# Half of four merge blocks issued beside the last attention rows, as a stream of lowest rank

## The chip, the cores and the metric

The kernel runs on one core of one Trainium2 chip. The metric is the device time of one execution in microseconds (us). Five engines work side by side, each on its own queue of instructions in program order: TensorE (PE: matrix products and transposes), VectorE (DVE), ScalarE (ACT), GpSimd (POOL) and SyncE (SP, which here issues most DMAs). They wait for one another through semaphores. A wait holds up everything behind it in the same queue.

## The reference, cut to what matters

One layer of a hybrid block over 512 tokens (528 with 16 meta tokens), width 1024, all in float32. Names as in the reference:

```
u = rmsnorm(h); proj = u @ w_in
gates  = sigmoid(proj[..., C_RW + C_FX:] + b_gate)
y_rw   = rwkv7_branch(...)     # recurrent half, 512 wide
y_fx   = fox_branch(...)       # causal attention with forget gates, 512 wide
merged = gates[:D] * (y_rw @ w_out_rw) + gates[D:] * (y_fx @ w_out_fx)
h = h + merged @ w_o
z = rmsnorm(h); h = h + square(relu(z @ w_up)) @ w_down
```

The change concerns `merged`: sixteen products of a 128-column block of `w_out_rw` or `w_out_fx` with one branch's output, each times its gate.

## The kernel before, in words

Every large product is made in three passes over operands that are split in two, `hi` (a rounded copy, made by ACT) and `lo` (the remainder, made by DVE): `hi*hi + hi*lo + lo*hi` (`passes`, `split`, `load_h`). A weight block is loaded by SP in two halves of 128x512 into `wraw` and split into `whi` and `wlo`; each of the three has a ring of four buffers.

*Front.* Up to the end of `turns.run()` the recurrent branch, the attention, the input projections and the sums of the later weights run as streams, Python generators that yield before a group of matmuls. `Turns.run` keeps a modelled PE time and takes the first stream, in order of rank, whose condition is met. That fixes the order of PE; the order on the other engines is fixed by the scheduler of the framework, which puts an instruction where its own model says that its inputs are ready. The gate blocks are the lowest projections: `gate_job` evacuates a product to `gt` and stores it to DRAM (`gates_d`, tile `gd`). Attention goes through four pairs of heads `p`, and in each through four rows of 128 queries `i`: `scored` (products `psc`, the mask and the row minimum on DVE, Exp on ACT, the scaling by `rsum` on DVE), `turned` (transposes `ppt`, `ppm`, copied to `pT`, `pTm`) and `mixed` (products `py`, copied to `y_fx`). For each row there are two heads, so two of each. `group_norm` ends the recurrent branch and writes `y_rw`.

*Merge.* After the front, `y_rw` and `y_fx` are split into `yhi`, `ylo` (eight blocks `k`, four of each branch). For each of eight output blocks `m` both weight halves are loaded, and for each branch `br` the gate is fetched (`gl`), ACT takes its Tanh, PE makes 12 matmuls into a PSUM bank `po` (4 blocks `k` by 3 passes), DVE multiplies, POOL adds the two branches, and the sum is split into `mhi`, `mlo`. That is 192 matmuls of 128x128 by 512 columns. The product with `w_o` follows (first `L1096`, then `L1113`), then the MLP (`L1143`, `L1233`).

`uhi`, `ulo` hold the normalised input, which only the projections read. Before, they live in a pool that ends with the front, and `yhi`, `ylo` take other memory (tags `zhi`, `zlo`).

Of the kernel before, what the change touches and what calls it, by code (L numbers as in the profile page):

```python
# [9 lines left out]
F32 = mybir.dt.float32  # L10
F32R = mybir.dt.float32r
# [15 lines left out]
KB = 8  # L27
CDEC = math.exp(-0.5)
SLICES = (4, 6, 6)
FIRST = (0, 4, 10)  # L30


# [118 lines left out]
class Turns:  # L151
# [1 line left out]

    ROOM = {0: 0.0, 1: 0.8, 2: 1.5, 3: 1.5, 4: 2.5, 8: 0.5, -1: 0.0}

    def __init__(self, tc, clock):
        self.tc, self.clock, self.streams, self.count = tc, clock, [], 0
# [29 lines left out]
def kernel(ctx, tc, ht, x, win, par, cst, gain, lora, wout, wo, wup, wdn, out, dbg=None):  # L189
# [6 lines left out]
    def dump(name, ap):  # L196
        if name in dbg:
            nc.sync.dma_start(dbg[name], ap)
# [60 lines left out]
    def split(hi, lo, x):  # L259
        A.copy(hi, x)  # L260
# [7 lines left out]
    quarters = [[wdn[i][256 * c:256 * c + 256] for c in range(8)] for i in range(4)]  # L268
    tsum = [[dr.tile([256, 512], F32, name=f"tsum{i}") for c in range(8)] for i in range(4)]

    with ExitStack() as st:
        up = st.enter_context(tc.tile_pool(name="up", bufs=1))
        ps = st.enter_context(tc.tile_pool(name="ps", bufs=2, space=PSUM))

        def ppj(name="ppj"):
# [160 lines left out]
            return job, raws  # L436

        converted = []

        def convert(job, raws):  # L440
            low = V if len(converted) < 2 else G
# [10 lines left out]
        def projections(total):  # L452
            fetched, done = None, 0
            while done < total:
                if fetched is None:
                    yield lambda: 0.0 if jobs else math.inf
                    fetched = fetch(jobs.pop(0))
                cur = convert(*fetched)
                fetched = fetch(jobs.pop(0)) if jobs else None
                while cur is not None:  # L460
                    (_, _, _, begin, parts, ev, need), w = cur
                    nxt = convert(*fetched) if fetched else None
                    fetched = fetch(jobs.pop(0)) if jobs else None
                    if need is not None:
                        yield need
                    evac = begin()
                    for a0, a1 in parts:
                        po = None
                        n = 0
                        for k in range(KB):  # L470
                            if k % 2 == 0 or a1 - a0 > 300:
                                yield lambda f=po is None: max(ck.ready(*w[k // 4]), ck.ring("pj", 1, 2) if f else 0.0)
                            if po is None:
                                po = ppj("pj")[:, :a1 - a0]
                            for a, b in passes(wk(w, k), U):
# [5 lines left out]
                    cur = nxt  # L481

        def gate_job(i):
            def begin():
# [514 lines left out]
        def weight_sums():  # L999

            def part(t, c):
                return t[c].rearrange("(a b) c -> a (b c)", b=2)

            def behind(dma, engine):
                x = next(x for x in reversed(nc.cur_bb.bb.instructions) if str(x.engine).endswith(engine) and x.name != dma.ins.name)
                tc.add_manual_dep(dma.ins, x.name, mybir.DependencyInfo(mybir.DependencyClass.NoSync, mybir.DependencyReason.DATA),
                                  reason="spread over the front")

            t1, t2, t3, t4 = tsum
            b11, b12, b22, b21 = quarters  # L1010
            steps = []
            for c in range(8):
                for a, b in (((t1, b11), (t1, b12)), ((t3, b12), (t3, b22)), ((t2, b22), (t2, t1)), ((t4, b21), (t4, t2))):
                    steps += [(*a, c, False), (*b, c, True)]
            for n in range(1, len(steps) - 2, 2):
                steps[n], steps[n + 1] = steps[n + 1], steps[n]
            for n, (dst, src, c, adds) in enumerate(steps):
                yield lambda: 45.0 + 6.0 * n
                if adds:
                    behind(nc.gpsimd.dma_start(part(dst, c), part(src, c), accum_op=ALU.add, max_dma_last_dim=2048), "Pool")  # L1020
                else:
                    behind(nc.scalar.dma_start(part(dst, c), part(src, c), max_dma_last_dim=2048), "Activation")
# [12 lines left out]
    hres = hp.tile([128, 4, 1024], F32, name="hres")  # L1035
    yhi = hp.tile([128, KB, S], F32R, name="yhi", tag="zhi")
    ylo = hp.tile([128, KB, S], F32R, name="ylo", tag="zlo")
    ps = ctx.enter_context(tc.tile_pool(name="ps2", bufs=4, space=PSUM))

    def ppo():  # L1040
# [4 lines left out]

    with ExitStack() as st:
        mp = st.enter_context(tc.tile_pool(name="mp", bufs=1))
        for j, src in enumerate((y_rw, y_fx)):
            for k in range(4):
                split(yhi[:, 4 * j + k, :], ylo[:, 4 * j + k, :], src[:, k, :])  # L1050
        mhi = mp.tile([128, KB, S], F32R, name="mhi")
        mlo = mp.tile([128, KB, S], F32R, name="mlo")
        for m in range(KB):
            w = load_w(wout[m])
            pp = []
            for br in range(2):
                g = mp.tile([128, S], F32, name=f"gl{br}", bufs=2)
                nc.sync.dma_start(g, gates_d[8 * br + m])
                act(g, g, AF.Tanh, scale=0.5)
                po = ppo()  # L1060
                n = 0
                for k in range(4 * br, 4 * br + 4):
                    for a, b in passes(wk(w, k), (yhi, ylo)):
                        mm(po, a, b[:, k, :], start=n == 0, stop=n == 11)  # L1064
                        n += 1
                V.scalar_tensor_tensor(g, g, 1.0, po, ALU.add, ALU.mult)
# [11 lines left out]
        zhi = hp.tile([128, KB, S], F32R, name="zhi", tag="zhi")  # L1078
        zlo = hp.tile([128, KB, S], F32R, name="zlo", tag="zlo")
        pin = pinned(merged)  # L1080
        early = []
        for j in range(2):
# [281 lines left out]
```

## Time and profile before

| what | us |
|---|---|
| median of three runs | 908.65 (905.33 to 912.98) |
| the profiled execution, its own time | 908.14 |
| its span, first to last instruction | 906.1 |
| PE busy in the span | 862.7 (95%) |
| matmuls of the merge (`L1064`), first start to last start | 479.39 to 523.39 |
| the last row of attention, its last product `py` | 476.83, takes 2.20 |

The 2.0 us between the span and the profiled execution's time lie around the first and last instruction. Times in the trace count from the start of the span. `PEclk` is the share of its clock that TensorE was granted. A row of a timeline gives start, duration, engine, line, operation, `out<-in`, sizes, and in brackets the idle time just before it with what ended it. Line numbers are those of the kernel before; in the changed kernel the lines behind the edit are larger by some.

### The profile page before, as it was taken

The page shows a single profiled execution, that of the slowest core. Times are in us where ns is not written, and L with a number is a line of the kernel's source. Part 1 is how long each engine was busy: PE and PEld are TensorE (multiplying, and loading weights), DVE is VectorE, ACT ScalarE, POOL GpSimd, SP SyncE. Part 2 cuts the span into 40 slices and gives each one's busy share as a digit, 9 for nine tenths or more (in the row PEclk, how much of TensorE's full clock was granted, in tenths as well). Part 3 has the DMA queues.
Part 4 walks back from the last instruction along what each step waited for, and adds up shares of the span by engine and source line. Part 5 has one row for each costly group of instructions (what it writes and reads, how often), then busy time and mean ns, then how long its engine had stood idle before and what let it go on. Part 6 is the DMA issues. An engine that isn't in the chain of part 4 may idle for free.

```text
span 906.1 us, 15737 instructions
## 1 busy us (share of the span) xinstructions
PE 862.7 (95%) x5896; PEld 702.6 (78%) x5896; DVE 594.3 (66%) x1168; ACT 462.1 (51%) x937; POOL 177.2 (20%) x169
## 2 busy tenths in 40 slices
PE   7889898999899999998989999999999999999998
PEld 6878786767797777676857877988888888888886
DVE  7965894447968794455476756377556675566776
ACT  7837243786355532675364644255444554344542
POOL 1154552223544353322301210000000000000000
PEclk9999998999999999999988999999999999999999
DMA  6223547475753467674685643034632366522564
GB/s 211 69 73 96 139 103 207 108 168 136 164 141 97 113 188 182 164 188 106 164 249 186 206 160 95 1 93 147 194 113 93 96 194 192 151 99 94 152 214 169
DMA packets 69771, 129.46 MB, mean 143 GB/s; under 512 B 6840, under 2 KB 7992, under 8 KB 69696
## 3 DMA queue, kind: packets, MB, share of 16 engines
q1 hardware_dynamic: 52288, 94.91, 32.9%
q0 software_dynamic: 8704, 16.78, 11.6%
q10 hardware_dynamic: 8704, 16.78, 5.6%
q8 instruction: 46, 0.75, 0.3%
q14 instruction: 29, 0.24, 0.1%
HBM read 122.13 MB, written 39.86 MB: 179 GB/s over the span
## 4 chain that ended last, share of the span: by engine, by line
PE 72%; DVE 15%; ACT 3%; issue 3%; DMA 2%; POOLq 0%; POOL 0%; ACTq 0%; SPq 0%; DVEq 0%
PE po L1143 19%; PE pj L476 16%; PE po L1233 12%; PE pd L1233 5%; PE po L1064 3%; PE po L1113 2%; PE pw L828 2%; DVE tmp L810 1%; PE psc L580 1%; PE py L625 1%; DVE AX L822 1%; PE pbt L776 1%; DVE Tt L822 1%; DVE AX L811 1%; DVE L L730 1%
## 5 line engine op out<-in xcount | busy, mean ns | idle before, releaser
L237 DVE TENSOR_TENSOR wlo<-wraw,whi 128x512 fp32r<-128x512 f32 x200 | 140.3, 708 | 95.8 <-ACT whi L236 95.5
L236 ACT CAST whi<-wraw 128x512 fp32r<-128x512 f32 x200 | 123.7, 621 | 135.8 <-PE po L1143 43.0
L476 PE MATMUL pj<-uhi,whi 128*128 128x264 f32 (+1 forms) x480 | 170.0, 354 | 11.0 <-DVE orr L307 3.9
L476 PE MATMUL pj<-ulo,whi 128*128 128x264 f32 (+1 forms) x480 | 157.5, 328 | 0.6 <-DVE ulo L390 0.6
L476 PE MATMUL pj<-uhi,wlo 128*128 128x264 f32 (+1 forms) x480 | 156.9, 327 | 0.0
L448 POOL TENSOR_TENSOR wlo<-wraw,whi 128x512 fp32r<-128x512 f32 x76 | 104.4, 1383 | 162.2 <-ACT whi L447 143.6
L476 PEld LDWEIGHTS pj<-uhi,whi 128*128 128x128 f32 x480 | 93.1, 194 | 32.7 <-issue 11.3
L476 PEld LDWEIGHTS pj<-uhi,wlo 128*128 128x128 f32 x480 | 93.4, 195 | 7.3
L476 PEld LDWEIGHTS pj<-ulo,whi 128*128 128x128 f32 x480 | 93.6, 195 | 5.4 <-DVE ulo L390 1.1
L1143 PE MATMUL po<-zhi,whi 128*128 128x512 f32 (+1 forms) x248 | 94.8, 382 | 0.0
L1143 PE MATMUL po<-zlo,whi 128*128 128x512 f32 (+1 forms) x248 | 94.8, 382 | 0.0
L1143 PE MATMUL po<-zhi,wlo 128*128 128x512 f32 (+1 forms) x248 | 94.8, 382 | 0.0
L447 ACT CAST whi<-wraw 128x512 fp32r<-128x512 f32 x80 | 49.2, 618 | 45.0 <-PE pj L476 27.3
L1233 PE MATMUL po<-wlo,fhi 128*128 128x512 f32 x160 | 62.4, 390 | 0.0
L1233 PE MATMUL po<-whi,flo 128*128 128x512 f32 x160 | 62.3, 389 | 0.0
L1233 PE MATMUL po<-whi,fhi 128*128 128x512 f32 x160 | 62.2, 389 | 0.0
L1143 PEld LDWEIGHTS po<-zhi,wlo 128*128 128x128 f32 x248 | 46.6, 188 | 9.1
L1143 PEld LDWEIGHTS po<-zlo,whi 128*128 128x128 f32 x248 | 46.6, 188 | 9.0
L1143 PEld LDWEIGHTS po<-zhi,whi 128*128 128x128 f32 x248 | 46.6, 188 | 8.9
L1155 ACT CAST fhi<-R 128x768 fp32r<-128x768 f32 (+1 forms) x32 | 30.2, 943 | 24.0 <-DVE R L1162 13.6
L1156 DVE TENSOR_TENSOR flo<-R,fhi 128x768 fp32r<-128x768 f32 (+1 forms) x32 | 34.8, 1089 | 7.8 <-ACT fhi L1155 7.8
L1233 PEld LDWEIGHTS po<-wlo,fhi 128*128 128x128 f32 x160 | 30.0, 188 | 6.5 <-DVE wlo L237 0.3
(292 smaller groups left out, 1658.9 us busy)
## 6 DMA issues: line engine op xcount, KB each, us to landing
wraw<-in_win SPq DMA_DIRECT2D x84, 256.0 KB, 3.0
tsum<-in_wdn ACTq DMA_DIRECT2D x32, 512.0 KB, 4.3
wraw<-in_wup SPq DMA_DIRECT2D x64, 256.0 KB, 2.6
wraw<-tsum SPq DMA_DIRECT2D x64, 256.0 KB, 2.8
wraw<-in_wdn SPq DMA_DIRECT2D x48, 256.0 KB, 2.7
tsum<-in_wdn POOLq DMA_DIRECT2D x16, 512.0 KB, 7.6
tsum<-tsum POOLq DMA_DIRECT2D x16, 512.0 KB, 6.3
gd<-gt SPq DMA_DIRECT2D x16, 256.0 KB, 2.3
```

Source lines behind the costliest of these rows:

```text
L236: A.copy(hi, raw)
L237: low.tensor_tensor(lo, raw, hi.bitcast(F32), ALU.subtract)
L447: A.copy(hi, raw)
L448: low.tensor_tensor(lo, raw, hi.bitcast(F32), ALU.subtract)
L476: mm(po, a, b[:, k, a0:a1], start=n == 0, stop=n == 23)
L822: V.tensor_copy(dst[rs_, :, o:o + 32], src[rs_, :, :n2].rearrange("p t n -> p n t"))
L828: mm(ps_[hs, n - b0, :], lhs(n)[hs], rhs(n)[hs], start=True, stop=True)
L1064: mm(po, a, b[:, k, :], start=n == 0, stop=n == 11)
L1143: mm(po[:, t0:t1], a, b[:, k, t0:t1], start=n == 0, stop=n == 23)
L1155: A.copy(fhi[:, j, a:b], R[:, a:b])
L1156: V.tensor_tensor(flo[:, j, a:b], R[:, a:b], fhi[:, j, a:b].bitcast(F32), ALU.subtract)
L1233: mm(x[i], a[:, k, left, 128 * i:128 * i + 128], c, start=start and k == 0 and n == 0, stop=stop and k == n_pairs - 1 and n == 2)
```

## The change

A new stream `merge_ahead` of rank 9, behind all others, runs in the front once all projections are out. It puts `yhi`, `ylo` into the memory of `uhi`, `ulo` (the pool `up` now lasts to the end, and `zhi`, `zlo` use it later), loads the recurrent half of `wout[0..3]` (`load_h`, so all four `whi` and `wlo` buffers are taken), fetches the four gates into new tiles `ge`, splits the four blocks of `y_rw`, and asks for 48 matmuls in groups of three (one `k`, one `m`) into four PSUM banks named `pe`, which are free by then. `k` runs outside and `m` inside, so all four products end with the last twelve. Behind the streams, ACT takes the Tanh of each `ge` and DVE multiplies it with its product. In the merge, blocks 0 to 3 then load and compute only their attention half (12 matmuls in place of 24). To make room in SBUF the scratch for descriptors of POOL's DMAs is set to 8192 bytes a partition in `kernel()`.

```diff
+EARLY = 4
-    ROOM = {0: 0.0, 1: 0.8, 2: 1.5, 3: 1.5, 4: 2.5, 8: 0.5, -1: 0.0}
+    ROOM = {0: 0.0, 1: 0.8, 2: 1.5, 3: 1.5, 4: 2.5, 8: 0.5, 9: 0.5, -1: 0.0}
...
+    up = ctx.enter_context(tc.tile_pool(name="up", bufs=1))
+    ge = [cp.tile([128, S], F32, name=f"ge{m}") for m in range(EARLY)]
     with ExitStack() as st:
-        up = st.enter_context(tc.tile_pool(name="up", bufs=1))
...
+        Y, early_po = [], []
+        def merge_ahead():
+            yield projected
+            Y.extend(up.tile([128, KB, S], F32R, name=name, tag=tag) for name, tag in (("yhi", "uhi"), ("ylo", "ulo")))
+            ws = [load_h(wout[m][:, :512], V, "w", (4, 4, 4)) for m in range(EARLY)]
+            for m in range(EARLY):
+                nc.sync.dma_start(ge[m], gates_d[m])
+            for k in range(4):
+                yield normalised[k // 2][1]
+                split(Y[0][:, k, :], Y[1][:, k, :], y_rw[:, k, :])
+            for m in range(EARLY):
+                early_po.append(ps.tile([128, 512], F32, name="pe", tag=("pj", "pj", "py", "ch")[m], bufs=(2, 2, 1, 1)[m]))
+            for k in range(4):
+                for m in range(EARLY):
+                    yield lambda: max(ck.ready(*ws[m]), ck.ready(*Y))
+                    for n, (a, b) in enumerate(passes([x[:, 128 * k:128 * k + 128] for x in ws[m]], Y)):
+                        mm(early_po[m], a, b[:, k, :], start=k == 0 and n == 0, stop=k == 3 and n == 2)
+        turns.add(9, merge_ahead())
...
             turns.run()
+        for g, po in zip(ge, early_po):
+            act(g, g, AF.Tanh, scale=0.5)
+            V.scalar_tensor_tensor(g, g, 1.0, po, ALU.add, ALU.mult)
...
         for m in range(KB):
-            w = load_w(wout[m])
-            pp = []
-            for br in range(2):
+            if m < EARLY:
+                w, pp = [None, load_h(wout[m][:, 512:], V, "w", (4, 4, 4))], [ge[m]]
+            else:
+                w, pp = load_w(wout[m]), []
+            for br in range(len(pp), 2):
...
-    nc = bacc.Bacc("TRN2", target_bir_lowering=False, num_devices=1)
+    nc = bacc.Bacc("TRN2", target_bir_lowering=False, num_devices=1, dynamic_dma_scratch_size=8192)
```

Three places show what this does to the order of the instructions. A row is line, operation, `out<-in`, size; `pe` as an output of a matmul is a bank of the new stream, `pe` as its input is a row of attention.

First, PE from the scores of the last row of attention (`i` = 3 of the last pair) on. Before:

```order
L580 MATMUL psc<-ka,qa 128x256 x2
L622 MATMUL py<-pTm,vm 64x128 x2
L625 MATMUL py<-pT,vt 64x128 x6
L609 MATMUL ppm<-cs,pe 16x128
L611 MATMUL ppt<-cs,pe 128x128 x4
```

Now, in the same place:

```order
L584 MATMUL psc<-ka,qa 128x256 x2
L1046 MATMUL pe<-yhi,whi 128x512
L1046 MATMUL pe<-ylo,whi 128x512
L1046 MATMUL pe<-yhi,wlo 128x512
...
L626 MATMUL py<-pTm,vm 64x128 x2
L629 MATMUL py<-pT,vt 64x128 x6
```

All 48 early matmuls stand behind these scores: 9 here, 9 behind the `py` of row 2, 6 between the two sets of transposes of row 3, 12 behind these, and 12 behind the last `py`. None stands ahead of the scores.

Second, ACT and DVE in row 2 of the last pair, ahead of those scores. ACT before, from the two `pTm` copies of row 1 to the second of the two Exp of row 2 (`pe,rsum`, 400 wide):

```order
L614 COPY pTm<-ppt 16x128 x2
L236 CAST whi<-wraw 128x512
L594 ACTIVATE pe,rsum<-pe,nm 128x400
L626 COPY y_fx<-py 128x128
L948 COPY yT<-pyt 64x256 x2
L236 CAST whi<-wraw 128x512
L594 ACTIVATE pe,rsum<-pe,nm 128x400
```

ACT now, over the same stretch:

```order
L618 COPY pTm<-ppt 16x128 x2
L261 CAST yhi<-y_fx 128x512
L237 CAST whi<-wraw 128x512
L261 CAST yhi<-y_rw 128x512
L261 CAST yhi<-y_fx 128x512
L237 CAST whi<-wraw 128x512 x2
L598 ACTIVATE pe,rsum<-pe,nm 128x400
L237 CAST whi<-wraw 128x512
L630 COPY y_fx<-py 128x128
L952 COPY yT<-pyt 64x256 x2
L261 CAST yhi<-y_fx 128x512
L598 ACTIVATE pe,rsum<-pe,nm 128x400
```

Ahead of the first Exp there were one cast and are now six (and two more of `yhi<-y_rw` ahead of the `yT` copies above this piece); between the two Exp there was one and are now two. On DVE the masked minimum of the second head (`ISA ... 128x400`) has moved behind the scaling of the first, with three more `wlo` ahead of it than before:

```order
L595 ISA pe,nm<-psc,nF_5379 128x400
L595 ISA nm 128x1
L238 TENSOR_TENSOR wlo<-wraw,whi 128x512 x2
L599 RECIPROCAL rsum<-rsum 128x1
L593 TENSOR_TENSOR psc<-psc,cs 128x128
L600 TENSOR_SCALAR pe<-pe,rsum 128x400
L238 TENSOR_TENSOR wlo<-wraw,whi 128x512
L595 ISA pe,nm<-psc,nF_5381 128x400
```

Before, it stood ahead of that scaling:

```order
L591 ISA pe,nm<-psc,nF_5375 128x400
L591 ISA nm 128x1
L589 TENSOR_TENSOR psc<-psc,cs 128x128
L237 TENSOR_TENSOR wlo<-wraw,whi 128x512
L595 RECIPROCAL rsum<-rsum 128x1
L591 ISA pe,nm<-psc,nF_5377 128x400
L591 ISA nm 128x1
L596 TENSOR_SCALAR pe<-pe,rsum 128x400
```

Third, DVE where the front hands over to the merge. Before:

```order
L613 COPY pT<-ppt 128x512
L261 TENSOR_TENSOR ylo<-y_fx,yhi 128x512 x2
L237 TENSOR_TENSOR wlo<-wraw,whi 128x512
L261 TENSOR_TENSOR ylo<-y_fx,yhi 128x512
L1066 SCALAR_TENSOR_TENSOR gl_5703<-gl_5703,po 128x512
```

Now:

```order
L617 COPY pT<-ppt 128x512 x2
L1057 SCALAR_TENSOR_TENSOR ge_124<-ge_124,pe 128x512
L262 TENSOR_TENSOR ylo<-y_fx,yhi 128x512
L1057 SCALAR_TENSOR_TENSOR ge_125<-ge_125,pe 128x512
L1057 SCALAR_TENSOR_TENSOR ge_126<-ge_126,pe 128x512
L1057 SCALAR_TENSOR_TENSOR ge_127<-ge_127,pe 128x512
L238 TENSOR_TENSOR wlo<-wraw,whi 128x512 x4
L1094 SCALAR_TENSOR_TENSOR gl_5788<-gl_5788,po 128x512
```

Before, the weights of the first merge blocks were split by then. Now the four `wlo` of the next weight halves stand behind the multiplications of all four early products.

Elsewhere the order of PE, DVE and POOL is as before up to this stretch. On ACT the four Tanh of `ge`, with two loads of a function table, stand in the front: three among the first gate blocks (about 142 to 153 us in the trace before), one at about 202 us. On SP the four loads of `ge` stand there too, each a few entries behind the store of its gate.

More of the change, by code (lines that the diff above doesn't have):

```diff
@@ L481, in projections @@
                     cur = nxt
+            projected.done = True
         def gate_job(i):
@@ L1035 @@
     hres = hp.tile([128, 4, 1024], F32, name="hres")
-    yhi = hp.tile([128, KB, S], F32R, name="yhi", tag="zhi")
-    ylo = hp.tile([128, KB, S], F32R, name="ylo", tag="zlo")
+    yhi, ylo = Y
     ps = ctx.enter_context(tc.tile_pool(name="ps2", bufs=4, space=PSUM))
@@ L1047 @@
         mp = st.enter_context(tc.tile_pool(name="mp", bufs=1))
-        for j, src in enumerate((y_rw, y_fx)):
-            for k in range(4):
-                split(yhi[:, 4 * j + k, :], ylo[:, 4 * j + k, :], src[:, k, :])
+        for k in range(4):
+            split(yhi[:, 4 + k, :], ylo[:, 4 + k, :], y_fx[:, k, :])
         mhi = mp.tile([128, KB, S], F32R, name="mhi")
@@ L1077 @@
             nc.sync.dma_start(hres[:, i, :], x[128 * i:128 * i + 128, :])
-        zhi = hp.tile([128, KB, S], F32R, name="zhi", tag="zhi")
-        zlo = hp.tile([128, KB, S], F32R, name="zlo", tag="zlo")
+        zhi, zlo = (up.tile([128, KB, S], F32R, name=name, tag=tag) for name, tag in (("zhi", "uhi"), ("zlo", "ulo")))
         pin = pinned(merged)
```

1 line of the change is left out of this document (added).

## The prediction

> **What bounds the kernel now.** I read the page first, then the stretches around the change, then the timelines of PE, ACT, DVE and SP in them.
>
> ```profile
> PE 862.7 (95%) x5896; PEld 702.6 (78%) x5896; DVE 594.3 (66%) x1168; ACT 462.1 (51%) x937; POOL 177.2 (20%) x169
> PE 72%; DVE 15%; ACT 3%; issue 3%; DMA 2%; POOLq 0%; POOL 0%; ACTq 0%; SPq 0%; DVEq 0%
> ```
>
> PE is busy for 95% of the span and 72% of the last chain, so moving matmuls gains only what PE loses at the new place. The stretches show how much that is:
>
> ```profile
> core 0: us, PE busy (x) PEld busy (x) DVE busy (x) ACT busy (x) POOL busy (x), PEclk, DMA share, GB/s
> 464.10:467.60 3.50, 1.39 (x8) 0.93 (x8) 3.29 (x10) 3.46 (x9) 0.00 (x0) 0.91 0.99 168
> 467.60:470.40 2.80, 2.80 (x13) 1.76 (x12) 1.73 (x8) 2.75 (x7) 0.00 (x0) 0.50 0.86 238
> 470.40:473.80 3.40, 2.37 (x20) 1.76 (x17) 3.38 (x13) 2.50 (x8) 0.00 (x0) 0.50 1.02 396
> 473.80:477.20 3.40, 2.77 (x15) 1.73 (x16) 3.19 (x7) 0.37 (x2) 0.00 (x0) 0.50 0.69 282
> 477.20:480.60 3.40, 3.04 (x19) 2.45 (x18) 2.19 (x4) 0.88 (x2) 0.00 (x0) 0.50 0.15 43
> 480.60:523.60 43.00, 43.00 (x191) 35.57 (x190) 29.10 (x39) 24.50 (x41) 10.45 (x7) 1.00 0.67 217
> ```
>
> Two things are lost here: PE is idle, most of it in the first stretch (1.39 of 3.50 busy), and from 467 to 480.6 it runs at half clock. The merge from 480.6 on has no gap (43.00 of 43.00). In the first stretch ACT (3.46) and DVE (3.29) are full: PE waits for them. The PE rows:
>
> ```profile
> 464.75 0.27 PE L609 MATMUL ppt<-cs,pe 128*16 128x128 f32 x1 [0.73 <-DVE pe L596]
> 466.81 0.27 PE L609 MATMUL ppt<-cs,pe 128*16 128x128 f32 x1 [1.46 <-DVE pe L596]
> 467.64 2.42 PE L580 MATMUL psc<-ka,qa 64*128 64x272 f32 x8
> 470.00 0.69 PE L622 MATMUL py<-pTm,vm 16*64 16x128 f32 x4
> 473.19 0.38 PE L609 MATMUL ppm<-cs,pe 128*16 128x128 f32 x1 [1.03 <-DVE pe L596]
> 475.06 0.37 PE L609 MATMUL ppm<-cs,pe 128*16 128x128 f32 x1 [0.63 <-DVE pe L596]
> 476.21 0.69 PE L622 MATMUL py<-pTm,vm 16*64 16x128 f32 x4
> 476.83 2.20 PE L625 MATMUL py<-pT,vt 128*64 128x128 f32 x16
> 479.39 0.79 PE L1064 MATMUL po<-yhi,whi 128*128 128x512 f32 x1 [0.35 <-ACT y_fx L626]
> 479.98 0.63 PE L1064 MATMUL po<-ylo,whi 128*128 128x512 f32 x1
> 480.41 0.49 PE L1064 MATMUL po<-yhi,wlo 128*128 128x512 f32 x1
> 480.73 0.39 PE L1064 MATMUL po<-yhi,whi 128*128 128x512 f32 x1
> 523.39 0.39 PE L1064 MATMUL po<-yhi,wlo 128*128 128x512 f32 x1
> ```
>
> The 480.73 row is the fourth of 192 matmuls and the 523.39 row the last: 188 steps in 42.66 us, 0.227 each at full clock; at half clock a step is 0.43 (479.98 to 480.41). The merge's last matmul is through at 523.6. Every wait in the list is for one row of attention's softmax.
>
> **The change, part by part.** The sum is made as the time at which the 192 matmuls are done, against 523.6.
>
> *1. The matmuls that leave.* 48 x 0.227 = 10.9 us leave the merge. They are not removed: they cost what they take at the new place, and all 48 stand behind `psc` of row 3. So the idle time ahead of it (0.73 + 1.46) is not filled.
>
> *2. Row 2 comes later.* ACT and DVE are full there, and the new order puts casts and subtractions ahead of the Exp.
>
> ```profile
> 459.34 0.69 ACT L487 ACTIVATE gt<-pj,pr 128x512 f32<-128x512 f32 x1 [0.85 <-ACT pe L594]
> 459.92 0.73 ACT L948 COPY yT<-pyt 64x256 f32<-64x256 f32 x2
> 460.92 0.53 ACT L614 COPY pTm<-ppt 16x128 f32<-16x128 f32 x2 [0.27 <-DVE pT L613]
> 462.87 0.63 ACT L594 ACTIVATE pe<-pe,nm 128x400 f32<-128x400 f32 x1 [0.78 <-DVE nm L591]
> 466.71 1.13 ACT L260 CAST yhi<-y_rw 128x512 fp32r<-128x512 f32 x2
> ```
>
> ACT now runs, from the end of `gt` at 460.0: two casts 1.13, `yT` 0.73, `pTm` 0.53, four casts at about 0.53: 464.5. Then two `whi` whose raw halves SP issued late:
>
> ```profile
> 460.94 0.40 SPq L233 DMA_DIRECT2D wraw<-in_wout  x1
> 462.07 0.33 SPq L233 DMA_DIRECT2D wraw<-in_wout  x1
> wraw<-in_wout SPq DMA_DIRECT2D x16, 256.0 KB, 3.9
> ```
>
> With 3.9 us to land, the raw half issued to 461.3 is there at 465.2: cast to 465.8. The first Exp runs from 465.8 instead of 462.87. Its sum is read at 466.6; `RECIPROCAL`, mask and scaling end at 467.4, a `wlo` (0.7) at 468.1, the second minimum (0.55) at 468.65, the second Exp at 469.4, behind it `yT`, `ylo`, `RECIPROCAL`, `y_rw` and the scaling on DVE:
>
> ```profile
> 463.70 0.55 DVE L591 CUSTOM_DVE_ANT_0 pe<-psc,nF 128x400 f32<-128x400 f32 x1
> 465.85 0.16 DVE L595 RECIPROCAL rsum<-rsum 128x1 f32<-128x1 f32 x1
> 466.24 0.42 DVE L596 TENSOR_SCALAR pe<-pe,rsum 128x400 f32<-128x400 f32 x1
> 467.04 0.68 DVE L237 TENSOR_TENSOR wlo<-wraw,whi 128x512 fp32r<-128x512 f32 x1
> ```
>
> That ends near 470.6, and the second set of transposes starts there instead of at 466.81. The same sum over the order before comes out 0.2 to 0.3 late, so I take 3.6 us: `psc` at 471.2 instead of 467.64. Bounds: 0, if the raw halves land early and ACT catches up, to 4.5, if the fourth (issued 462.07) is late too.
>
> *3. From `psc` to the last `py`.* At half clock `psc` takes 2.36 (467.64 to 470.00): 473.6. Nine matmuls at 0.43: 477.4. I take the clock to be back at 477.2, after the first stretch 473.8 to 477.2 that is filled with 128x128 matmuls. The rest at full clock: `py` of row 2 (470.00 to 472.16, halved) 1.1, nine matmuls 2.0, transposes 0.6, six 1.4, transposes 0.6, twelve 2.7, last `py` (476.21 to 479.03, halved) 1.4: 9.8, so 487.1. The softmax of row 3 takes 5.1 us from the end of `psc` (470.0) to the second scaled row (475.06) and now has 7 us of matmuls over it: its waits (1.03 + 0.63) go.
>
> *4. The hand-over.* Twelve early matmuls 2.7: 489.8. Three of the merge that need no `wlo`: 490.5. The first `wlo` stands behind the multiplication of the last early product: 489.8 + 0.69 + 0.68 + hops 0.2 = 491.4. PE waits 0.9, where it waited 0.35 for `y_fx`. Bounds 0.4 and 2: the four `whi` casts ahead of it could be late.
>
> *5. The rest.* 144 - 3 = 141 matmuls x 0.227 = 32.0: done at 523.4, against 523.6. Terms 1 to 5 give **-0.2**.
>
> *6. End of the merge.* The next product waits for PSUM banks that the gates' multiplications free:
>
> ```profile
> 525.62 0.50 PE L1096 MATMUL po<-whi,mhi 128*128 128x512 f32 x1 [0.48 <-DVE gl L1066]
> 526.82 0.50 PE L1096 MATMUL po<-whi,mhi 128*128 128x512 f32 x1 [0.23 <-DVE gl L1066]
> ```
>
> With four gates fewer to fetch this lag of 0.71 may go, or the blocks of 2.7 us instead of 5.4 may keep it: 0 to -0.7, I take **-0.3**.
>
> *7. The front.* ACT gets two table loads and four Tanh, SP four loads with a wait for the gate's store.
>
> ```profile
> L255 ACT ACT_TABLE_LOAD x13 | 16.7, 1283 | 0.2
> L1059 ACT ACTIVATE gl<-gl 128x512 f32<-128x512 f32 x16 | 10.0, 631 | 14.2 <-DMA gl<-gd 12.6 <-DVE wlo L237 1.4
> 147.34 0.62 ACT L447 CAST whi<-wraw 128x512 fp32r<-128x512 f32 x1 [4.18 <-DMA wraw<-in_win]
> 204.30 0.74 ACT L875 COPY uv<-pvt 64x256 f32<-64x256 f32 x2 [2.06 <-PE pvt L873]
> ```
>
> 1.28 + 0.63 = 1.91 fits into the 4.18 and into the 2.06 of idle ACT time where they now stand. The second and third Tanh wait for a load that SP issues only once the gate's store has landed; behind them wait the Exp of another pair's rows 0 and 1. I take **+0.2**, between 0 and, all on PE's path, 2 x 1.28 + 4 x 0.63 = 5.1. The halved scratch of POOL's DMAs I cost at 0; no row shows it.
>
> Four Tanh and four gate loads fewer in the merge cost or gain nothing: ACT is busy 24.50 of 43.00 there. `zhi` in the place of `yhi` waits for the same matmuls as before.
>
> Sum: 908.14 - 0.2 - 0.3 + 0.2 = 907.84, **907.8 us**. The profiled execution stands 0.5 below the median of 908.65.
>
> The clock is the term to doubt. In the rows PE is busy for 2.80 of 2.80 up to 470.4 and the clock stays at 0.50; it comes back after a stretch with 3.04 of 3.40 that ends in 128x128 matmuls. The Trainium skill, "TensorE: Matmul & The Clock Gate", section "Part 1: The HAM clock gate (the 'warmup' mystery)", says that one busy window of about 3.4 us brings the full clock back. By that rule the changed kernel would have it from about 473.8, and the sum would be 906.0; the trace before does not agree, since its full window to 470.4 brought nothing back.
>
> On term 7 the Trainium skill, "ScalarE: Activation LUTs", section "What ACT_TABLE_LOAD costs", adds a drain of about 1.38 us to each table switch. By it the load at 204.30 would overrun its gap by about 1.2 and the sum would be 909.0; thirteen loads here have 0.2 us of idle time ahead of them in all, so I keep 1.28.
>
> **The rivals.**
>
> *The clock is back one stretch earlier*, at 473.8, because `psc` and the transposes now fill 470.7 to 473.8. Then the nine matmuls take 2.0 instead of 3.9: 1.8 less, **906.0**. For it: the 3.04 of 3.40 that released it. Against: the full stretch to 470.4 that did not.
>
> *Row 2 is not held up*, the two raw halves landing before ACT comes to them: `psc` at 467.64 and 3.6 less, **904.2**. For it: ACT's casts at 464.5 to 466.7 in the trace before did not wait visibly. Against: the order, which puts six casts ahead of the Exp wherever the data are.
>
> *The clock stays at half until 480.6*, four stretches as before: 3.4 us at half speed, 1.7 more, **909.5**.
>
> *The front stops on the gates*, the one on the other side: the Tanh of the third `ge` (`ge_126`) waits on ACT for a load that SP issues behind three weight loads, and the Exp behind it feed transposes on PE. It decides if that load lands more than 3 us after the `pTm` copies were due; price up to 5.1, **913.0**. Against: no wait of PE for ACT's Exp or `pTm` in the rows I read there.
>
> *The change does nothing*: out, the order shows the matmuls moved.
>
> **How the numbers follow.** Forecast (about level, 906.5 to 909) 0.42; clock earlier 0.2; row 2 not held up 0.1; clock later 0.13; front 0.1; others 0.05. Their times run from 904.2 to 913.0, and single runs of the kernel before lie 3.3 below and 4.3 above their median; cutting a tenth at each end gives 903.5 to 912.5. A measurement of this kernel can tell about 1% (9 us) from no change. Faster by that needs 899: even 10.4 us, all that PE loses from 464.1 to 480.6, would just do it: 0.03. Slower by that needs 917, more than any one rival: 0.05. Within: 0.92.
>
> **What would show it.** Right: the first Exp of row 2 three us later behind `whi` casts; a longer wait of PE ahead of the last `psc`; no waits in row 3; about 1 us of PE idle behind the last early matmul, for a `wlo`; half clock for about three stretches instead of four. Wrong: `psc` near 467.6, a hand-over wait over 2 us, or any new PE wait for `ge` near 150 or 204.

## The result and the profile after

| | us |
|---|---|
| the changed kernel, median of four runs | 921.66 (919.60 to 924.19) |
| the kernel before, median of four runs | 908.50 (905.33 to 912.98) |
| ratio | 1.0122, 95% interval 1.0084 to 1.0159 |
| the profiled execution, its own time and its span | 923.65, 921.8 |

The forecast was 907.8, about level. The kernel became slower: by the ratio 11.1 us, between 7.6 and 14.4. The profiled execution is one of the slower two of four, and its span is 15.7 us longer than that of the kernel before.

The page of the changed kernel, its busy line and its last chain:

```profile
PE 866.9 (94%) x5896; PEld 705.7 (77%) x5896; DVE 590.1 (64%) x1168; ACT 464.5 (50%) x939; POOL 177.0 (19%) x169
PE 67%; DVE 15%; DMA 6%; ACT 4%; issue 3%; POOL 1%; POOLq 0%; SPq 0%; ACTq 0%; DVEq 0%
```

PE's share of the chain fell from 72% to 67%, and DMA's rose from 2% to 6%: transfers now end waits that they did not end before. Where, the timelines tell if the same matmul is looked up in both (up to the last row of attention the order of PE is the same). Its delay against the kernel before:

| the same place on PE | before | after | later by |
|---|---|---|---|
| transposes of the first attention row, first head | 151.88 | 157.30 | 5.42 |
| the same, second head | 152.10 | 158.37 | 6.27 |
| the next `psc` | 154.66 | 165.81 | 11.15 |
| first `py` | 159.18 | 173.18 | 14.00 |
| a projection matmul at the end of the front | 422.19 | 433.71 | 11.52 |
| `psc` of row 3 | 467.64 | 485.10 | 17.46 |
| end of the matmuls ahead of the wait for `gl` (start less wait) | 525.14 | 539.03 | 13.89 |
| the matmul behind that wait | 525.62 | 541.32 | 15.70 |
| end of the span | 906.1 | 921.8 | 15.7 |

So the change has four places: +8.58 in the front (0.85 at the second head's transposes and 7.73 from there to the first `py`), +5.94 in row 2, -3.57 from there through the merge, +1.81 at the product with `w_o`. The other 5.42 are there before the first of them, and 2.48 are made up again up to 422, both where the two kernels run the same order on PE. The experiments below show that the 5.42 differ between executions, so the 15.7 of the two spans are more than the 11.1 by the times.

*The front.* The timelines of SP, ACT and PE in the changed kernel, in order of time. SP issues the load of the third gate at 157.10, behind three weight loads; ACT comes to its Tanh and stops there for 8.15 us. Behind it in ACT's queue stand the two `pTm` copies, which read `ppt` and so free the PSUM banks that the next `psc` takes:

```profile
148.23 1.28 ACT L1056 ACT_TABLE_LOAD   x1
149.53 0.63 ACT L1056 ACTIVATE ge<-ge 128x512 f32<-128x512 f32 x1
154.63 2.43 SPq L436 DMA_DIRECT2D wraw<-in_win  x3
157.10 0.74 SPq L1036 DMA_DIRECT2D ge<-gd  x1
164.98 0.63 ACT L1056 ACTIVATE ge<-ge 128x512 f32<-128x512 f32 x1 [8.15 <-DMA ge<-gd]
165.52 0.52 ACT L618 COPY pTm<-ppt 16x128 f32<-16x128 f32 x2
165.81 1.55 PE L584 MATMUL psc<-ka,qa 64*128 64x272 f32 x4 [4.81 <-ACT pTm L618]
```

The 0.85 ahead of this have the same cause: at 154.89 the Tanh of the second gate had waited 0.73 for its load, with the Exp of the first row behind it. The tile's view gives the time from issue to landing of the four gate loads, the chain of work that ended last (followed from 150 to 170) has the third of them as a piece, and the stretches show what followed:

```profile
DMA to landing us min/median/max: 2.6/5.2/7.9
```

```profile
157.10 7.86 DMA ge<-gd
```

```profile
core 0: us, PE busy (x) PEld busy (x) DVE busy (x) ACT busy (x) POOL busy (x), PEclk, DMA share, GB/s
158.20:161.60 3.40, 2.62 (x53) 2.09 (x53) 2.09 (x6) 0.00 (x0) 0.03 (x1) 1.00 1.00 193
161.60:165.00 3.40, 0.00 (x0) 0.00 (x0) 0.00 (x0) 0.02 (x1) 0.00 (x0) 1.00 0.62 219
165.00:168.40 3.40, 2.59 (x7) 1.70 (x8) 1.21 (x5) 1.47 (x5) 0.00 (x0) 0.51 0.49 152
168.40:171.80 3.40, 3.40 (x17) 2.78 (x17) 1.48 (x6) 2.12 (x7) 2.10 (x2) 0.50 0.32 13
```

While the load is under way the DMA engines are full for one stretch (1.00) and 0.62 busy in the next. In that next stretch PE, DVE, ACT and POOL stand still, and then TensorE gets half its clock for 6.8 us. Of the delay of 7.73, 4.88 are there when `psc` starts (its wait is 4.81); nearly all the rest is the half clock, about 2.8 us.

*Row 2.* SP, ACT and PE of the changed kernel. The cast of `whi` between the two Exp waits 3.00 us for its raw half (a weight half as loaded, `wraw`), and with it the copy `y_fx` behind it:

```profile
471.39 0.33 SPq L492 DMA_DIRECT2D gd<-gt  x1
471.81 10.34 SPq L234 DMA_DIRECT2D wraw<-in_wout  x7
480.45 0.62 ACT L237 CAST whi<-wraw 128x512 fp32r<-128x512 f32 x1 [3.00 <-DMA wraw<-in_wout]
480.98 0.26 ACT L630 COPY y_fx<-py 128x128 f32<-128x128 f32 x1
481.29 0.38 PE L613 MATMUL ppt<-cs,pe 128*16 128x128 f32 x1 [4.17 <-ACT y_fx L630]
484.16 0.37 PE L613 MATMUL ppt<-cs,pe 128*16 128x128 f32 x1 [1.85 <-DVE pe L600]
485.10 2.23 PE L584 MATMUL psc<-ka,qa 64*128 64x272 f32 x8
```

PE waits 4.17 and 1.85 where it waited 0.73 and 1.46. Two shorter waits that were not there before stand ahead of these: 1.05 for `yT` at 473.08 and 0.70 at 476.50.

*From there on.* The clock is at half for three stretches instead of four, and row 3 has no waits. The hand-over waits 1.22, and the product with `w_o` 2.29 instead of 0.48. DVE's rows ahead of each are shown with them; `ge` is the tile of an early product, `gl` of one in the merge:

```profile
479.10:482.50 3.40, 1.02 (x4) 0.62 (x4) 1.40 (x4) 2.01 (x6) 0.00 (x0) 0.50 0.91 278
482.50:485.90 3.40, 1.74 (x8) 1.33 (x9) 3.14 (x8) 1.61 (x6) 0.00 (x0) 0.50 0.55 146
485.90:489.30 3.40, 3.40 (x13) 2.31 (x10) 2.48 (x10) 0.98 (x3) 0.00 (x0) 0.50 1.01 406
489.30:492.80 3.50, 3.50 (x27) 2.48 (x26) 1.86 (x7) 1.09 (x3) 0.00 (x0) 1.00 0.37 152
```

```profile
502.76 1.88 DVE L1057 SCALAR_TENSOR_TENSOR ge<-ge,pe 128x512 f32<-128x512 f32 x3
504.78 0.47 PE L1092 MATMUL po<-yhi,whi 128*128 128x512 f32 x1 [1.22 <-DVE ge L1057]
539.98 0.69 DVE L1098 SCALAR_TENSOR_TENSOR mlo<-gl,mhi 128x512 fp32r<-128x512 f32 x1 [1.03 <-ACT mhi L1097]
540.59 0.68 DVE L1094 SCALAR_TENSOR_TENSOR gl<-gl,po 128x512 f32<-128x512 f32 x1
541.32 0.50 PE L1123 MATMUL po<-whi,mhi 128*128 128x512 f32 x1 [2.29 <-DVE gl L1094]
```

### The profile page after: what moved, and what is told of

It is laid out like the page before. It is cut to its first block, busy times and chain, and to the rows that moved or that the text cites. A ratio compares the mean times of both kernels' runs of the same rounds, so it can differ in the third digit from the quotient of the medians.

```text
span 921.8 us, 15727 instructions
## 1 busy us (share of the span) xinstructions
PE 866.9 (94%) x5896; PEld 705.7 (77%) x5896; DVE 590.1 (64%) x1168; ACT 464.5 (50%) x939; POOL 177.0 (19%) x169
## 4 chain that ended last, share of the span: by engine, by line
PE 67%; DVE 15%; DMA 6%; ACT 4%; issue 3%; POOL 1%; POOLq 0%; SPq 0%; ACTq 0%; DVEq 0%
PE po L1170 19%; PE pj L479 16%; PE po L1260 10%; PE pd L1260 5%; PE po L1140 2%; PE psc L584 1%; DVE tmp L814 1%; DMA wraw<-in_wout 1%; PE pw L832 1%; PE py L629 1%; PE pe L1046 1%; DVE AX L826 1%; DVE wlo L238 1%; PE pbt L780 1%; DVE Tt L826 1%
## 5 line engine op out<-in xcount | busy, mean ns | idle before, releaser
L238 DVE TENSOR_TENSOR wlo<-wraw,whi 128x512 fp32r<-128x512 f32 x200 | 137.5, 695 | 99.5 <-ACT whi L237 99.2
L479 PE MATMUL pj<-uhi,whi 128*128 128x264 f32 (+1 forms) x480 | 171.9, 358 | 12.4 <-DVE orr L309 3.9
L479 PE MATMUL pj<-ulo,whi 128*128 128x264 f32 (+1 forms) x480 | 159.4, 332 | 0.8 <-DVE ulo L392 0.8
L479 PE MATMUL pj<-uhi,wlo 128*128 128x264 f32 (+1 forms) x480 | 158.8, 331 | 0.0
```

Source lines behind the costliest of these rows:

```text
L238: low.tensor_tensor(lo, raw, hi.bitcast(F32), ALU.subtract)
```

## The experiments

Line numbers differ by a few between the kernels. Every ratio is to the kernel before, measured beside it on the same chip; 0.001 is 0.9 us. The twelve kernels were measured in three rounds on two chips, in which the kernel before had medians of 910.85, 912.17 and 910.44, so the ratios are to be compared, not the medians.

| kernel | median, us | ratio to before | 95% interval |
|---|---|---|---|
| scratch_only | 913.19 | 1.0024 | 0.9997 to 1.0050 |
| gates_only | 916.48 | 1.0068 | 1.0043 to 1.0094 |
| gates_late | 914.62 | 1.0045 | 1.0022 to 1.0068 |
| store_act | 919.49 | 1.0094 | 1.0068 to 1.0120 |
| late_store | 912.95 | 1.0016 | 0.9994 to 1.0037 |
| before_store | 908.96 | 0.9976 | 0.9953 to 1.0000 |
| m_outer | 911.91 | 0.9994 | 0.9969 to 1.0019 |
| m_outer_gl3 | 908.61 | 0.9964 | 0.9940 to 0.9989 |
| early3_gl3 | 907.13 | 0.9966 | 0.9938 to 0.9994 |
| early2 | 908.01 | 0.9949 | 0.9926 to 0.9972 |
| early2_gl3 | 905.80 | 0.9934 | 0.9903 to 0.9964 |
| early2_poolw | 907.45 | 0.9974 | 0.9952 to 0.9996 |

The theory after the result: the largest cost is the front, where a gate load stops ACT; then row 2, where a weight load does; the moved matmuls themselves save what was forecast. The rival: the front is late for another reason (the halved scratch, or the DMA load), since the profile was already 5.5 us late at 103 us (the `psr` at 103.25 before starts at 108.72 now).

**scratch_only** is the kernel before with

```diff
-    nc = bacc.Bacc("TRN2", target_bir_lowering=False, num_devices=1)
+    nc = bacc.Bacc("TRN2", target_bir_lowering=False, num_devices=1, dynamic_dma_scratch_size=8192)
```

> The kernel before with one edit, the descriptor scratch of POOL's DMAs at 8192 bytes. The changed kernel was already 5.3 us later than the kernel before at 103 us of its span, ahead of the first moved instruction. Theory 1 (the scratch costs nothing, that early lag is the scatter of the clock's half-speed stretches from execution to execution): within 2 us of the kernel before, 906.5 to 910.5. Rival (the halved scratch delays the weight sums and with them other transfers): 3 to 5 us slower, 911.5 to 913.5.

Measured: 1.0024, interval from 0.9997, so 0 to 4.5 us by the interval; its profile has a span of 906.9, 0.8 longer. A cost of 3 us or more isn't excluded by the times alone, but the profile has no place for it: its largest delay on PE up to 422 us is 1.8.

**gates_late** is the changed kernel with the gates held back on both queues:

```diff
-                nc.sync.dma_start(ge[m], gates_d[m])
+                ld = nc.sync.dma_start(ge[m], gates_d[m])
+                x = next(x for x in reversed(nc.cur_bb.bb.instructions) if str(x.engine).endswith("SP") and x.name != ld.ins.name)
+                tc.add_manual_dep(ld.ins, x.name, ...)
...
-            act(g, g, AF.Tanh, scale=0.5)
+            after(act(g, g, AF.Tanh, scale=0.5), exps[-1])
```

> The changed kernel, but the four ge loads stand on SP behind the early wout loads, and their Tanh on ACT behind the last Exp, instead of in the front. Theory 1 (the wait of the third ge Tanh at 156.8 to 165.0 and the half clock behind it cost 4.8 + 2.8 = 7.6 us): about 914, PE's wait ahead of psc at 165.8 gone, lag at 250 us at most 6. Rival (the front would have been late by other causes, such as the scratch or the DMA load): 919 to 922, the lag at 250 us still over 10.

Measured: 1.0045 against 1.0122 for the changed kernel, 0.0077 or 7.0 us less, where 7.6 were expected. The intervals of the two kernels are apart. The wait at 165 is gone; at 245 us of the profile before PE is 2.2 late, and of this nothing arises in the front (1.2 late at 151.88 and at 204). Row 2 and the end are as in the changed kernel: the hand-over waits 1.29, and row 2 has the PE rows

```profile
468.68 0.38 PE L615 MATMUL ppt<-cs,pe 128*16 128x128 f32 x1 [3.99 <-ACT y_fx L632]
471.56 0.37 PE L615 MATMUL ppt<-cs,pe 128*16 128x128 f32 x1 [1.85 <-DVE pe L602]
```

**gates_only** tests the same from the other side, the gates alone, in the kernel before:

```diff
+        def fetch_gates():
+            yield projected
+            for m in range(4):
+                nc.sync.dma_start(ge[m], gates_d[m])
+        turns.add(9, fetch_gates())
...
             turns.run()
+        for g in ge:
+            act(g, g, AF.Tanh, scale=0.5)
...
-                g = mp.tile([128, S], F32, name=f"gl{br}", bufs=2)
-                nc.sync.dma_start(g, gates_d[8 * br + m])
-                act(g, g, AF.Tanh, scale=0.5)
+                if br == 0 and m < 4:
+                    g = ge[m]
+                else:
+                    g = mp.tile([128, S], F32, name=f"gl{br}", bufs=2)
+                    nc.sync.dma_start(g, gates_d[8 * br + m])
+                    act(g, g, AF.Tanh, scale=0.5)
```

> The kernel before with one part of the change alone: the first four gates are fetched into ge tiles and get their Tanh in the front, where the scheduler puts them as in the changed kernel (and the scratch at 8192 to make room). No matmul is moved, y is split where it was, and the merge takes these four gates instead of fetching them. Theory 1 (the front's wait for the third gate is the largest cost of the change and needs nothing of the rest): 6 to 8 us slower than the kernel before, with a PE wait of 4 to 5 us ahead of psc near 160. Rival (the wait arises only together with the memory or the DMA load of the moved work): within 2 us of the kernel before.

Measured: 1.0068, 6.2 us slower (3.9 to 8.6), with not one matmul moved. ACT and PE give the same picture as in the changed kernel, with a wait a little under the 4 to 5 expected:

```profile
159.81 0.63 ACT L1042 ACTIVATE ge<-ge 128x512 f32<-128x512 f32 x1 [7.04 <-DMA ge<-gd]
160.63 1.55 PE L584 MATMUL psc<-ka,qa 64*128 64x272 f32 x4 [3.70 <-ACT pTm L618]
```

Both directions agree: the front's cost is the early gates, 6 to 7 us, and needs nothing else of the change but, at most, the halved scratch, which gates_only has too (both kernels of the first direction have it). The profiles say the same: from the first transposes to 165 us of the profile before, PE falls behind by 8.6 us in the changed kernel, by 8.0 in gates_only, and by nothing in gates_late.

**store_act** and **late_store** take the last gate's store off SP, in the changed kernel and in gates_late. That store waits on SP for `gt`, and three of the four early weight loads stand behind it:

```diff
-                    nc.sync.dma_start(gates_d[i], gt)
+                    (nc.scalar if i == 15 else nc.sync).dma_start(gates_d[i], gt)
```

> The changed kernel with the last gate stored from ACT's queue alone, the gates in the front as they were. Theory 1 (the two costs are apart and add up): 3 to 4 us less than the changed kernel, 917.5 to 918.5, the 4.8 us wait at 165 still there. Rival (row 2 is bounded by ACT and DVE work): 920 to 922.

> gates_late with one more edit: the last gate is stored from ACT's queue instead of SP's, so the early wout loads no longer stand behind that store on SP. Theory 1 (row 2 is late because the fourth raw half is issued late, so that its cast waits 3.0 us on ACT ahead of the second Exp): the waits of PE ahead of the transposes of row 2 fall from 4.2 + 1.9 to under 3 together, 3 to 4 us less than gates_late, about 910 to 911. Rival (row 2 is late because ACT and DVE have too much work there, whatever lands when): within 1.5 us of gates_late, the waits still over 5 together.

Measured: store_act 1.0094, 2.5 us less than the changed kernel; late_store 1.0016, 2.6 less than gates_late. Both are a little under the 3 to 4 expected, and equal: the two costs are apart and add up. In each of the two pairs the intervals overlap, but the profiles agree: from 460 us of the profile before to `psc` of row 3, PE falls behind by 6.1 us in the changed kernel and 5.9 in gates_late, by 3.5 in store_act and 3.2 in late_store. In late_store the two Exp follow each other with no cast between, and the two waits of PE are one of 1.51:

```profile
472.34 0.63 ACT L600 ACTIVATE pe<-pe,nm 128x400 f32<-128x400 f32 x1
472.96 0.61 ACT L600 ACTIVATE pe<-pe,nm 128x400 f32<-128x400 f32 x1
474.24 0.38 PE L615 MATMUL ppt<-cs,pe 128*16 128x128 f32 x1 [1.51 <-DVE pe L602]
467.58 1.84 PE L586 MATMUL psc<-ka,qa 64*128 64x400 f32 x4 [1.60 <-ACT yT L954]
```

The edit does two things that these runs do not separate. It brings the second and third early load forward, and the scheduler puts the fourth one's cast ahead of the first Exp. The fourth load itself is not issued sooner: 2.7 us after the end of `gt` in the changed kernel (474.02 after 471.37), 3.0 in late_store (468.33 after 465.31). In the kernel's code `gt` takes a buffer of the ring of `wraw`; that the fourth load waits until the store has freed this buffer would fit, but no run tests it.

What stays is a wait of 1.60 for `yT`, which stands on ACT behind `y_rw`'s casts. late_store and gates_late have the same order on PE up to here, yet their first 103 us are not alike:

```profile
0.00:103.00 103.00, 88.22 (x598) 75.12 (x599) 74.19 (x147) 63.78 (x123) 32.41 (x42) 0.94 0.36 111
```

That is late_store; the same stretch of gates_late:

```profile
0.00:103.00 103.00, 87.39 (x637) 74.93 (x638) 78.20 (x154) 64.94 (x125) 35.77 (x45) 0.98 0.38 116
```

At a granted clock of 0.94 late_store gets through 598 matmuls, gates_late at 0.98 through 637. So the 5.5 us that the changed kernel was late at 103 us differ between executions of the same order, by where the clock's half stretches fall. Over all thirteen later profiles the delay at this place runs from -0.5 to 5.5 us, and it is 1.2 in scratch_only. The rival falls for the early lag.

**before_store** makes the same edit in the kernel before.

> The kernel before with the last gate stored from ACT's queue, nothing moved. Theory 1 (in the kernel before the wout loads behind that store delay nothing that PE waits for, since its casts did not wait visibly): within 1 us of the kernel before. Rival (the store holds up the weights there too, and what late_store gained belongs to any kernel): 2 to 3 us faster than before.

Measured: 0.9976, up to 1.0000, so 2.2 us faster, between the two theories and nearer to the rival. In its profile row 2 isn't faster: its two waits are 1.77 and 0.23 and a wait of 0.17 stands ahead of `psc`; what is shorter is the half clock after 467, three stretches instead of four. Whether the store or the phase of the clock does that, this run does not settle.

**m_outer** is late_store with the loops swapped:

```diff
-            for k in range(4):
-                for m in range(EARLY):
+            for m in range(EARLY):
+                for k in range(4):
```

> late_store with the two loops of the early matmuls swapped: m outside, k inside, so a product and its weight buffer are done every 12 matmuls and not all four at the end. Theory 1 (the wait of 1.29 us of the first merge matmul is for PSUM banks that the four multiplications free one after another at the very end): that wait falls under 0.7 us, and 0.5 to 1.5 us less than late_store in time, about 911.5. Rival (the multiplication of the last product alone sets the bank's release): the wait stays at 1.2 to 1.3 us and the time within 0.5 us of late_store, 913.

**m_outer_gl3** adds to m_outer a third buffer for `gl0` and `gl1`:

```diff
-                g = mp.tile([128, S], F32, name=f"gl{br}", bufs=2)
+                g = mp.tile([128, S], F32, name=f"gl{br}", bufs=3)
```

> m_outer with three instead of two buffers for each of gl0 and gl1. Theory 1 (the wait of 2.0 to 2.9 us ahead of the product with w_o comes from the last gate loads, which wait for a gl buffer two blocks back, and with half blocks two blocks are only 5.4 us): the wait falls to 0.7 us or less, 1.5 to 2 us less than m_outer, about 909.5 to 910. Rival (DVE is late there because of the splits of wup that stand ahead of it): the wait stays over 1.7 us and the time within 0.7 us of m_outer.

**early2** is m_outer with `EARLY = 2`, **early2_gl3** and **early3_gl3** have the third buffer and two or three blocks.

> m_outer with only two merge blocks' recurrent half in the stream (24 matmuls, two gates, two early weight halves). Theory 1 (the moved work costs by the casts and subtractions that it adds to ACT and DVE in row 2, and its gain comes from the first 24 matmuls, which cover the waits of row 3): PE's waits in row 2 fall by another 1 us against m_outer, the hand-over stays about as it was, time 1 to 2 us less than m_outer, about 910. Rival (more matmuls beside attention are better, the clock comes back through them): 1 to 3 us more than m_outer.

> early2 with three gl buffers. Theory 1 (half blocks make the gate ring late; with only two of them there is little left to gain): 0 to 1 us less than early2, 907 to 908. Rival (the ring still costs as with four blocks): 2 us or more less than early2, 906 or below.

> early2_gl3 with three merge blocks in the stream, 36 matmuls. Theory 1 (each block beyond the second adds two casts and two subtractions to row 2 and covers nothing more): between early2_gl3 and m_outer_gl3, 0.5 to 1.5 us more than early2_gl3. Rival (the number of blocks does not matter once the ring is deeper): within 0.5 us of early2_gl3.

Measured: m_outer 0.9994, 2.0 us less than late_store, more than expected, but its wait at the hand-over only fell from 1.29 to 0.87: neither theory's number, and the intervals of the two runs overlap. The waits ahead of the product with `w_o`, one line of the waits view from each of m_outer, m_outer_gl3, early3_gl3, early2 and early2_gl3, in this order (sum, times, longest):

```profile
PE po L1128 <- DVE gl L1099: 2.3, 2, 2.1
```

```profile
PE po L1128 <- DVE gl L1099: 2.2, 2, 2.0
```

```profile
PE po L1128 <- DVE gl L1099: 1.8, 1, 1.8
```

```profile
PE po L1128 <- DVE gl L1099: 0.6, 2, 0.3
```

```profile
PE po L1128 <- DVE gl L1099: 0.2, 1, 0.2
```

The third buffer did not shorten that wait (2.3 to 2.2), so the theory of the gate ring falls, and of the rival its main point holds: DVE is late there. m_outer_gl3's DVE shows it:

```profile
522.78 0.68 DVE L1099 SCALAR_TENSOR_TENSOR gl<-gl,po 128x512 f32<-128x512 f32 x1
525.90 0.69 DVE L1103 SCALAR_TENSOR_TENSOR mlo<-gl,mhi 128x512 fp32r<-128x512 f32 x1 [1.84 <-ACT mhi L1102]
526.51 0.68 DVE L1099 SCALAR_TENSOR_TENSOR gl<-gl,po 128x512 f32<-128x512 f32 x1
```

The multiplication at 526.51 that PE waits for needs nothing of the `mlo` ahead of it, but stands behind it, and `mlo` waits for POOL's sum and ACT's `mhi` of the block before, which began with the multiplication at 522.78. The rival's cause, the splits of `wup`, is neither shown nor excluded: four of their subtractions (`we`) stand on DVE between 513.61 and 521.06. The two kernels have this order on DVE alike (before, 524.27 and 524.88), so what differs is how late it runs; that four half blocks leave less time for the same sums and casts is my reading of it. With two the wait is 0.6, and the kernel is 0.9949 (early2): the number of blocks decides, as the dose shows (2.2, 1.8, 0.2 us for four, three, two with three buffers). That m_outer_gl3 took 3.3 us less than m_outer in its median (2.7 by the ratios), where the rival has at most 0.7, has no place in its rows; the two intervals overlap, and I count it as open.

early2 is 4.1 us less than m_outer by the ratios (1 to 2 expected). Its rows gain 1.7 at `w_o` and 0.5 at the hand-over, but the sum of its two waits ahead of the transposes of row 2 is 2.0, against 1.64 in m_outer. The waits did not fall as expected, yet row 2 got shorter: from `psc` of row 2 (467.00 in m_outer, 466.36 in early2) to the first of these transposes it took 6.69 us and then 5.31, and both transposes wait for DVE:

```profile
473.69 0.38 PE L615 MATMUL ppt<-cs,pe 128*16 128x128 f32 x1 [1.64 <-DVE pe L602]
```

```profile
471.67 0.28 PE L615 MATMUL ppt<-cs,pe 128*16 128x128 f32 x1 [1.65 <-DVE pe L602]
```

m_outer was at half clock there and early2 was not, so PE came later to the same wait in m_outer; a wait alone does not tell how late the engine behind it is. With half the early casts and subtractions row 2 is thus about 1.4 us shorter, and with 1.7 and 0.5 this makes 3.6 of the 4.1.

early2_gl3 is the best version, 0.9934 (0.9903 to 0.9964), 6.0 us less than before; the step from early2 is 1.4, inside the intervals. Of the 6.0 us the store accounts for 2.2 if its gain in before_store carries over, which leaves about 3.8 for the moved matmuls and the third buffer. early3_gl3 lies 2.9 above early2_gl3, as expected in sign, larger in size; their intervals overlap. early2_gl3's PE rows:

```profile
470.68 0.28 PE L615 MATMUL ppt<-cs,pe 128*16 128x128 f32 x1 [1.64 <-DVE pe L602]
485.69 0.50 PE L1097 MATMUL po<-yhi,whi 128*128 128x512 f32 x1 [0.35 <-ACT y_fx L632]
```

There is no wait in row 3, the hand-over is back at the 0.35 of before, and the 1.60 for `yT` stands as in late_store. Only one stretch of half clock is left, 472.40 to 475.80:

```profile
472.40:475.80 3.40, 3.40 (x12) 2.19 (x11) 3.01 (x11) 1.10 (x4) 0.00 (x0) 0.50 1.01 286
475.80:479.20 3.40, 3.40 (x26) 2.44 (x25) 3.40 (x10) 1.78 (x6) 0.00 (x0) 1.00 1.00 380
```

**early2_poolw** makes the two early `wlo` on POOL:

```diff
-            ws = [load_h(wout[m][:, :512], V, "w", (4, 4, 4)) for m in range(EARLY)]
+            ws = [load_h(wout[m][:, :512], G, "w", (4, 4, 4)) for m in range(EARLY)]
```

> early2 with the lower halves of the two early weight blocks made on POOL, which is idle in row 2, instead of on DVE. Theory 1 (what is left of the delay of row 2, PE waits of 1.6 and 1.65 us, is ACT's casts ahead of yT and the Exp): within 0.7 us of early2, the waits as they were. Rival (DVE is as full as ACT there): 0.7 to 1.5 us less than early2, the wait ahead of the transposes under 1.2 us.

Measured: 0.9974, against 0.9949 for early2 with overlapping intervals. The wait ahead of the transposes fell to 0.77, as the rival has it, the 1.60 for `yT` stayed, and the time did not fall. In its profile three stretches are at half clock there where early2 has one, and PE came later to that wait: from `psc` of row 2 to the second set of transposes it took 7.17 us (464.19 to 471.36), in early2 6.28 (466.36 to 472.64). So the shorter wait is no gain, and what POOL does for the row can't be told from the clock's phase. The run is inconclusive.

## Why the prediction was wrong, step by step

1. *The matmuls that leave.* Right. 48 left, all behind `psc` of row 3, and the idle time ahead of it was not filled.

2. *Row 2.* Right in kind, too small: 5.94 later, where 3.6 was taken and 4.5 was the upper bound. The bound allowed a late fourth raw half, but not what stood behind its cast besides the Exp: `y_fx`, which the first transposes wait for. The 3.9 us to land is the median of sixteen loads; the fourth half was issued at 474.02 and its cast began at 480.45, 6.4 later. The excess hangs on the store `gd<-gt` on SP ahead of the weight loads, which was visible in the timeline of SP before and wasn't counted. Moving it gave 2.5 and 2.6 us and left row 2 at 3.5 and 3.2, near the 3.6.

3. *From `psc` to the last `py`.* Right in its sum: half clock for three stretches; the last `py` ended about 15.5 after `psc` (499.53 + 1.09 less 485.10), forecast 15.9. The waits of row 3 went. Part of it is luck: the clock was back 4.2 us after `psc` began (489.30), not 6.0 (477.2 less 471.2), since the half clock had set in 6.0 us ahead of `psc` (479.10), not 4.2.

4. *The hand-over.* The size was near (1.22, forecast 0.9), the cause not: PE did not wait for a `wlo`, but for the PSUM banks that the four multiplications free, ahead of it.

5. *The rest.* Right: -3.57 from `psc` of row 3 through the merge, forecast -3.8 (3.6 + 0.2).

6. *The end of the merge.* Wrong in sign: +1.81, forecast -0.3. The working saw that four gates need less to be fetched. It did not follow DVE's queue: the multiplication stands behind `mlo`, which came later. The number of early blocks sets it (2.2, 1.8 and 0.2 us); why DVE runs later there is argued, not tested.

7. *The front.* This step made the prediction wrong. It took +0.2, with 5.1 as the end, and measured are 8.58 in the profile (7.73 of them at the third gate), 7.0 by taking the gates away, 6.2 by making only them. It named the right instruction as a rival (the Tanh of the third `ge` behind a load that SP issues late), gave it 0.1, and priced it by the busy time of the inserted instructions. But the price of an instruction that waits in an in-order queue is its data's arrival: the load landed 7.9 us after its issue, behind three weight loads on the same queue and with the DMA engines full (1.00). The trace before had the row to read, the time to landing of the weight load that SP issued there at 152.26:

```profile
DMA to landing us min/median/max: 7.0/7.0/7.0
```

Against the rival, it said that no PE wait for `pTm` stood in the rows before; that told nothing about a Tanh that was not there yet. And the half clock that an idle stretch brings, about 2.8 us here, was not in the bound, though it was in the sum for 467 to 480. The outcome, 11.1 us slower, lies where the prediction put 0.05, as more than any one rival: it is the front, the excess of row 2 and the end of the merge together.

The 0 for the scratch is not refuted: 0 to 4.5 us by its interval, 0.8 by its profile's span. On the table load the rows side with 1.28: at 148.23 the load, at 149.53 the Tanh, no idle time between.

## What to carry over

A cheap instruction put early in an in-order queue costs what its data take to arrive, and everything queued behind it pays: for each moved wait, find the issue of its transfer, how full the DMA engines are there, and the next instruction of that queue that PE needs. Bound it by that and by the half clock that an idle stretch brings, not by its busy time. And move as much as covers the waits, no more: here two blocks covered row 3, and the third and fourth only made ACT and DVE late.

## What the runs showed of the hardware that was not expected

One idle stretch of 3.4 us (161.60 to 165.00, 0.00 busy) was followed by 6.8 us at half clock, and the clock came back after a stretch that was full: 168.40 to 171.80 and 485.90 to 489.30, 3.40 of 3.40 each, as in early2_gl3 after 475.80. The Trainium skill, "TensorE: Matmul & The Clock Gate", "Part 1: The HAM clock gate (the 'warmup' mystery)", says that the clock is back after at least one busy window of about 3.4 us; in these rows one was enough. The kernel before has a row where one was not:

```profile
142.70:146.10 3.40, 3.40 (x10) 2.16 (x10) 0.94 (x6) 0.46 (x1) 1.94 (x2) 0.50 0.95 274
146.10:149.50 3.40, 3.40 (x29) 2.52 (x28) 0.49 (x4) 2.00 (x6) 1.41 (x2) 0.50 0.33 122
```

A full stretch at half clock, and the next at half clock too. The other way round, the kernel before had its clock back at 480.60 after a stretch that was not full (3.04 of 3.40). What tells these cases apart, no run here shows.

The four loads of `ge`, 256 KB each, landed between 2.6 and 7.9 us after their issue, in one kernel.
